# A hybrid decoder layer on one core: other PSUM pools for the projections, a rotary swap by transfers, a third plain FFN tile

## The chip, the cores and the metric

The kernel runs on one core of a Trainium2 chip. The metric is the device time of one execution in microseconds (us). Times of before are the median of three runs; the profile is of one further execution. Engines: PE (TensorE, matmuls), DVE (VectorE), ACT (ScalarE), POOL (GpSimd), SP (SyncE, whose queue issues the DMAs).

## The reference

One decode step plus a prompt of 1024 positions through one layer (all in float32). The prompt and the 8 decode positions are handled as one matrix of 1032 columns.

```python
def mixer_prompt(xn, w_in, w_out, ...):
    qkv, z, xbc, dt_raw = split_mix(xn @ w_in)
    for g, (window, dil) in enumerate(ATTN_PATTERNS):      # 3 patterns, dilation 1, 4, 16
        q = rope(qkv[..., g, 0, :, :], pos)
        k = rope(qkv[..., g, 1, :, :], pos)
        o, lse = dilated_window_prompt(q, k, qkv[..., g, 2, :, :], dil)
...
    attn = merge_patterns(outs, lses)                      # softmax over the three lse
    xs, Bm, Cm, dt, A = ssd_branch_inputs(causal_conv_silu(xbc_pad, ...), dt_raw, dt_bias, a_log)
    y, h_new = ssd_chunked(xs, dt, A, Bm, Cm)              # 8 chunks x 2 groups
    ssm = ssd_gate_out(y, xs, z, d_skip, ssd_norm_w)       # y * silu(z), RMSNorm
    return concatenate([attn, ssm], -1) @ w_out, ...
...
    yp = yp + rmsnorm(mix, norm_mix_post[l])
    yp = yp + rmsnorm(swiglu(rmsnorm(yp, norm_ffn_pre[l]), w_ffn_in[l], w_ffn_out[l]), norm_ffn_post[l])
```

The decode positions go the same way, with attention over the cached keys (`mixer_sample`), and the caches are copied to the outputs.

## The kernel before, in words

**Products.** Weights and activations are each split into a high and a low part; a product is three matmuls (high by high, low by high, high by low) for each of 8 slices of the inner dimension. One *unit* (`unit`, line 168, matmul on line 175) is these 24 matmuls into one accumulator of 344 columns; a weight tile has three units, for the column ranges c = 0, 1, 2. `gps` (line 182) gives the accumulators, going in turn through the list `gpools` of PSUM pools. In the three attention patterns and in z that list is `[psg]`, two buffers. `gemm` (line 189) loads a weight tile and runs its units; an ACT copy takes each accumulator out (line 586 in the patterns, into the tile `rw`).

**Stages, in order of units.** The conv projections XBC (units 0 to 36), attention patterns 0, 1, 2 (36 to 72, 72 to 108, 108 to 144), z (144 to 168), the output projection and its norms (168 to 204), the plain tiles of the FFN (from 204), its Strassen-like tiles (`blocks`, matmuls on line 1206: a tile of 1032 columns by 7 products of 12 matmuls of 258 columns, for each of two halves), the second FFN product and the tail.

**A pattern** is 12 weight tiles: for each of four pairs of heads (hp) v, q and k (`do_v`, `do_qk`), then `attend`, 8 steps j. `do_qk` swaps the rotary halves: four ACT copies of 32 x 1032 (line 615) make `sw` from `rw`, POOL multiplies it with the sines (line 616), DVE multiplies `rw` with the cosines (617) and adds both (620, 621). In `attend` the transposed probabilities go from PSUM to `pt` by ACT in 24 of the steps (line 671), else by DVE (673).

**Beside the patterns** run the SSD (`ssd`, from line 475; 16 groups: 8 chunks by 2) and the decode scores (`dec_scores(g)`, lines 731 to 757, after pattern g in the code). An SSD group loads `xg`, `bg` and the broadcast sums `e` (1 x 512 KB), and on DVE makes `xdt` (500), `xdd` (501), `gm` (507), 8 subtractions on `e` (516), `e*gm` (519), `eb*yo` (534), `xg+yp` (536) and `hst+stp` (542). All its PSUM tiles (`xt`, `gb`, `yp`, `yo`, `stp`), those of `dec_scores` (`rtp`, `stp`), and `pnp` and `wtp` (line 842) come from `side_ps`, the pool pss of two buffers. The *merge* of the patterns (lines 842 to 860) weights the three outputs and gives the attention part of the output projection its input.

**The norm stage.** `att_part(c)` adds the attention part to the output projection and lays two steps in the list `ahead`: `Norms.first` (statistics, first RMSNorm, residual) and `Norms.second` (second RMSNorm, the FFN's input `fh`, `fl`). They are carried out a number of units later, which the table `GAP` sets (line 27); so plain FFN tiles on c = 0, 1 run while the norm of c = 2 is worked out. `x_sums` and `w_blocks` (lines 1131 to 1190) make the sums and weight combinations that the Strassen-like tiles need.

**Order.** A scheduler sets each engine's program order when the kernel is built, from dependencies and priorities (`prio`: evac, w, side, late, main). The pools, though, hand out buffers in code order: a tile gets the buffer of the tile that was taken from its pool two before it in the code (with two buffers), and may be written only when that one's last reader is done.

Of the kernel before, what the change touches and what calls it, by code (L numbers as in the profile page):

```python
# [26 lines left out]
GAP = ((1, 3), (1, 4), (2, 6))  # L27
# [22 lines left out]
def trunk(tc, a, o):  # L50
# [558 lines left out]
    def do_qk(g, hp, which):  # L609
        rw = proj_raw(g * 12 + 4 * which + hp)  # L610
        with prio("side"):
            sw = swpp.tile([P, 3 + T], F32, tag="swp", name="sw")
            for q in range(4):
                s = q ^ 1
                nc.scalar.copy(sw[q * 32:(q + 1) * 32, 0:T], rw[s * 32:(s + 1) * 32, :])  # L615
            nc.gpsimd.tensor_tensor(out=sw[:, 0:T], in0=sw[:, 0:T], in1=sin, op=ALU.mult)  # L616
            nc.vector.tensor_tensor(out=rw, in0=rw, in1=cos, op=ALU.mult)
            qp = krp if which else qrp
            qr = qp.tile([P, S], F32, tag="qr", name="qr")
            nc.vector.tensor_tensor(out=pview(qr, g), in0=porder(rw, g), in1=porder(sw, g), op=ALU.add)  # L620
# [314 lines left out]
    gpools.append(psa)  # L935
# [54 lines left out]
    def stat(x, first, acc):  # L990
        if first:
            nc.scalar.activation(out=acc, in_=x, func=AF.Square)
# [12 lines left out]
    class Norms:  # L1005
# [12 lines left out]
        def first(self, prev):  # L1018
            c0, c1 = self.c0, self.c1
            with prio("evac"):  # L1020
                r = np_.tile([P, CW], F32, tag="nr", name="nr", bufs=1)
                finish(self.acc, r, prev=prev)
                self.acc = np_.tile([P, CW], F32, tag="nacc", name="nacc2")
                self.h = []
                for i in range(3):
# [4 lines left out]
                    for m in range(3 * i, 3 * i + n):  # L1030
                        mv, h = mix[m][:, c0:c1], self.h[m]
                        nc.vector.tensor_tensor(out=mv, in0=mv, in1=r, op=ALU.mult)
                        nc.vector.scalar_tensor_tensor(out=h, in0=mv, scalar=nw(MIX_POST, m), in1=h, op0=ALU.mult,  # L1033
                                                       op1=ALU.add)
                        stat(h, m == 0, self.acc)
                    nc.sync.dma_start(out=h_d[3 * i:3 * i + n, :, c0:c1].rearrange("k p t -> p k t"), in_=x[:, :n])

        def second(self, prev):
            c0, c1 = self.c0, self.c1
            with prio("evac"):  # L1040
                r = np_.tile([P, CW], F32, tag="nr", name="nr2", bufs=1)
                finish(self.acc, r, prev=prev)
                for m in range(KT):
# [4 lines left out]
                    nc.vector.tensor_tensor(out=fl[m][:, c0:c1], in0=mv, in1=fh[m][:, c0:c1], op=ALU.subtract)  # L1048
# [9 lines left out]
    def att_part(c):  # L1058
# [9 lines left out]
        ahead.extend([(GAP[c][0], nm.first), (GAP[c][1], nm.second)])  # L1068
# [5 lines left out]
    att_part(2)  # L1074
# [18 lines left out]
    def plain(t, c, w):  # L1093
# [5 lines left out]
        with prio("evac"):  # L1099
            s = np_.tile([P, T], F32, tag="fs", name="fs", bufs=2)[:, :CW]  # L1100
            nc.scalar.activation(out=s, in_=pg, func=AF.Silu)
# [48 lines left out]
    wslots = [(mixp, "mix")] * 8 + [(whp, "wh"), (wlp, "wl"), (whp, "wh"), (wlp, "wl")]  # L1150
# [45 lines left out]
    def blocks(t, s, w):  # L1196
# [26 lines left out]
        with prio("evac"):  # L1223
            add(u2, p1, b)
        b = prod("b22")
        with prio("evac"):
            add(v, u2, b)
        b = prod("t3")
        with prio("evac"):
            add(u3, u2, b)  # L1230
        b = prod("t4")
        with prio("evac"):
            next_copy(add(up[:, 0], u3, b))
        b = prod("t1")
        with prio("evac"):
            add(gate[:, 1], v, b)
            add(up[:, 1], u3, b)
# [10 lines left out]
    def hid_load(t):  # L1248
        with prio("w"):
            hr = np_.tile([P, T], F32, tag="xr", name="hr", bufs=3)  # L1250
# [10 lines left out]
    def ffn_out(gi):  # L1261
# [36 lines left out]

        def ev(m, c, ps):
# [20 lines left out]
        def put(c, m, r):  # L1320
# [3 lines left out]
            nc.vector.tensor_tensor(out=fv, in0=fv, in1=r, op=ALU.mult)  # L1324
# [12 lines left out]
        for c, (c0, c1) in enumerate(CL):  # L1337
            for m in range(KT):
# [30 lines left out]
    for t in range(2, HT):  # L1369
        w = w_blocks(t)  # L1370
# [101 lines left out]
```

## Time and profile before

| what | value |
|---|---|
| runs, us | 1889.53, 1892.22, 1893.98; median 1892.22 |
| profiled execution, us | 1887.21; its span on the core 1885.4 |
| granted TensorE clock, mean | 0.975 |
| PE, DVE, ACT, POOL busy, us | 1776.3, 1151.1, 781.9, 323.0 |
| last eight SSD groups, start of their xdt, us from start | 433.8 to 555.9 |
| dec_scores(0), first copy of its rows to its stp, us from start | 573.66 to 603.84 |
| last projection of z | 967.7 |
| norm stage (first att_part to first Strassen-like product) | 1037 to 1209 |

The page of the profile gives busy time by engine, the span in 40 slices, the DMA queues, the chain that ended last, the costliest groups of instructions and the DMA issues. A row of a group reads: line, engine, operation, output and inputs by tile name, shape, count, busy time, mean duration in ns, the idle time just before and who ended it. The views of windows give busy time by engine (with the number of instructions), the granted clock and the DMA share for a stretch.

### The profile page before, as it was taken

What the parts mean: (1) busy time and instruction counts of PE and PEld (TensorE: products, weight loads), DVE (VectorE), ACT (ScalarE), POOL (GpSimd) and SP (SyncE); (2) the same over time, 40 slices, a digit from 0 to 9 for tenths busy, and PEclk for the clock granted to TensorE, in tenths of its full rate; (3) what the DMA queues carried; (4) which work ended last, traced back from release to release, by engine and by line L of the source; (5) the groups of instructions that cost most, each with busy time, mean ns of one, the idle gap of its engine ahead of it and who ended that gap; (6) DMA issues with size and microseconds to landing.
All of it is one profiled execution on the core that took longest, in us unless ns stands there. A gap on an engine that the chain in (4) does not pass through costs nothing.

```text
span 1885.4 us, 30770 instructions
## 1 busy us (share of the span) xinstructions
PE 1776.3 (94%) x12207; PEld 1658.5 (88%) x12207; DVE 1151.1 (61%) x2247; ACT 781.9 (41%) x1436; POOL 323.0 (17%) x218
## 2 busy tenths in 40 slices
PE   8999989999998899999789995999999999999995
PEld 6999877888887788988678995899999999999995
DVE  6545667677765544456676699766666665532338
ACT  5533454555554555565242345432232232531133
POOL 0000244544224311133542210000000000000020
PEclk9999999999999999999979998999999999999998
DMA  4322333443325333445755443354544445886686
GB/s 158 133 95 83 104 118 117 139 135 114 99 88 180 114 118 108 148 160 192 190 148 163 128 160 124 118 174 170 171 165 170 172 162 184 314 295 205 214 305 202
DMA packets 135056, 298.61 MB, mean 158 GB/s; under 512 B 18416, under 2 KB 85200, under 8 KB 133504
## 3 DMA queue, kind: packets, MB, share of 16 engines
q1 hardware_dynamic: 134912, 296.64, 47.6%
q8 instruction: 96, 1.57, 0.3%
q14 instruction: 48, 0.39, 0.1%
HBM read 247.49 MB, written 137.10 MB: 204 GB/s over the span
## 4 chain that ended last, share of the span: by engine, by line
PE 38%; DVE 7%; DMA 3%; issue 1%; ACT 1%; POOL 1%; SPq 0%; DVEq 0%; POOLq 0%; ACTq 0%
PE fb L1206 21%; PE g L175 15%; DMA nt<-n_d 2%; PE pg L175 1%; POOL nt L855 1%; DMA hr<-hid_d 1%; DVE xr L1033 1%; PE pu L175 1%; DVE nt L856 1%; DVE nacc L996 1%; DVE sl L925 0%; DVE wl L164 0%; DVE mix L1045 0%; DVE nt L857 0%; DVE fl L1048 0%
## 5 line engine op out<-in xcount | busy, mean ns | idle before, releaser
L175 PE MATMUL g<-xh,wh 128*128 128x344 f32 x1344 | 442.9, 330 | 9.2 <-ACT rw L586 4.9
L175 PE MATMUL g<-xl,wh 128*128 128x344 f32 x1344 | 439.8, 327 | 1.5 <-DVE xl L231 1.5
L175 PE MATMUL g<-xh,wl 128*128 128x344 f32 x1344 | 438.4, 326 | 0.5 <-DVE wl L164 0.5
L175 PEld LDWEIGHTS g<-xh,wh 128*128 128x128 f32 x1344 | 255.3, 190 | 18.9 <-ACT rw L586 7.3
L175 PEld LDWEIGHTS g<-xh,wl 128*128 128x128 f32 x1344 | 255.6, 190 | 12.3 <-issue 11.0
L175 PEld LDWEIGHTS g<-xl,wh 128*128 128x128 f32 x1344 | 255.6, 190 | 10.6 <-issue 7.7
L1206 PE MATMUL fb<-fh,wsl 128*128 128x258 f32 x1280 | 234.6, 283 | 0.9 <-DVE wsl L1176 0.8
L1206 PEld LDWEIGHTS fb<-fh,wsl 128*128 128x128 f32 x1280 | 198.0, 189 | 1.5 <-DVE wsl L1176 0.9
L1206 PE MATMUL fb<-fl,wsl 128*128 128x258 f32 x640 | 180.8, 283 | 0.0
L164 DVE TENSOR_TENSOR wl<-wr,wh 128x1024 fp32r<-128x1024 f32 (+1 forms) x93 | 114.1, 1227 | 82.6 <-ACT wh L163 82.4
L175 PE MATMUL g<-hh,wh 128*128 128x344 f32 x432 | 137.4, 320 | 0.7 <-ACT wh L163 0.7
L175 PE MATMUL g<-hh,wl 128*128 128x344 f32 x432 | 137.7, 319 | 0.2 <-DVE wl L164 0.2
L175 PE MATMUL g<-hl,wh 128*128 128x344 f32 x432 | 137.3, 320 | 0.0
L163 ACT CAST wh<-wr 128x1024 fp32r<-128x1024 f32 (+1 forms) x93 | 92.5, 995 | 106.6 <-PE g L175 97.3
L660 ACT ACTIVATE sm<-sm,ngm 128x128 f32<-128x128 f32 (+1 forms) x192 | 84.9, 443 | 107.5 <-DVE ngm L656 99.5
L1288 POOL TENSOR_TENSOR ow<-wr,ow 128x512 fp32r<-128x512 f32 x8 | 10.2, 1299 | 686.3 <-ACT ow L1287 686.3
L1206 PEld LDWEIGHTS fb<-fl,wsl 128*128 128x128 f32 x640 | 120.9, 189 | 0.0
L616 POOL TENSOR_TENSOR sw<-sw,sin 128x1032 f32<-128x1032 f32 x24 | 75.8, 3157 | 250.8 <-ACT sw L615 187.3
L615 ACT COPY sw<-rw 32x1032 f32<-32x1032 f32 x96 | 101.0, 1052 | 1.4
L1210 DVE TENSOR_TENSOR fo<-fp,fb 128x258 f32<-128x258 f32 x160 | 63.7, 419 | 57.4 <-PE fb L1206 57.2
L586 ACT COPY rw<-g 128x344 f32<-128x344 f32 x108 | 47.2, 443 | 113.2 <-PE g L175 70.6
L175 PEld LDWEIGHTS g<-hh,wh 128*128 128x128 f32 x432 | 80.9, 188 | 1.1 <-ACT wh L163 1.0
(362 smaller groups left out, 3759.7 us busy)
## 6 DMA issues: line engine op xcount, KB each, us to landing
out_skv<-in_cache SPq DMA_DIRECT2D x64, 1023.5 KB, 5.5
wr<-in_w_in SPq DMA_DIRECT2D x56, 512.0 KB, 3.7
out_skv<-in_cache SPq DMA_DIRECT2D x16, 1022.0 KB, 5.5
wr<-in_w_out SPq DMA_DIRECT2D x24, 512.0 KB, 3.6
hr<-hid_d SPq DMA_DIRECT2D x22, 516.0 KB, 5.0
hid_d<-fo SPq DMA_DIRECT2D x40, 258.0 KB, 3.1
wg<-in_w_fin SPq DMA_DIRECT2D x20, 512.0 KB, 5.5
wu<-in_w_fin SPq DMA_DIRECT2D x20, 512.0 KB, 3.6
```

The lines of the kernel that those rows point to most:

```text
L163: nc.scalar.copy(wh[:, :cols], wr[:, :cols])
L164: nc.vector.tensor_tensor(out=wl[:, :cols], in0=wr[:, :cols], in1=wh[:, :cols], op=ALU.subtract)
L175: last = nc.tensor.matmul(ps, x[:, ws], y[:, c0:c1], start=(k == 0 and j == 0), stop=(k == n - 1 and j == 2))
L586: return nc.scalar.copy(rw[:, c0:c1], ps)
L615: nc.scalar.copy(sw[q * 32:(q + 1) * 32, 0:T], rw[s * 32:(s + 1) * 32, :])
L616: nc.gpsimd.tensor_tensor(out=sw[:, 0:T], in0=sw[:, 0:T], in1=sin, op=ALU.mult)
L660: nc.scalar.activation(out=sm[:, h, :nk], in_=sm[:, h, :nk], func=AF.Exp, scale=SCALE, bias=ngm[:, g, j, i:i + 1], accum_out=den[:, g, j, ...
L855: nc.gpsimd.tensor_tensor(out=nt, in0=nt, in1=wt, op=ALU.mult)
L856: nc.vector.tensor_tensor(out=nt[:, 0], in0=nt[:, 0], in1=nt[:, 1], op=ALU.add)
L996: nc.vector.tensor_tensor(out=acc, in0=acc, in1=sq, op=ALU.add)
L1206: nc.tensor.matmul(ps, x[:, ks], y, start=(k == 0 and j == 0), stop=(k == 3 and j == 2))
L1210: return nc.vector.tensor_tensor(out=dst, in0=x, in1=y, op=ALU.add)
```

## The change

- In the code ahead of `dec_scores(0)` the list of accumulators is set to `[psg, psg, pss, pss]`, and after z to `[psg, psa]`. So in patterns 1 and 2 and in z two of four accumulators in a row come from pss.
- The rotary swap is by four DMAs on SP's queue in place of the four ACT copies, and the sine product moves from POOL to DVE.
- All copies to `pt` are on ACT.
- `Norms.first` is cut in two (`first`, `resid`); `GAP` has three numbers a range; the residual's first statistic stands behind the last silu; `x_sums` and the first `w_blocks` are issued after the last norm.
- Three plain tiles in place of two; the Strassen-like ones start at t = 3.
- In `blocks` the product t1 comes after t2, no longer last; the weight slots `wslots` start with the other pools; the first two `hid_load` take another pool; the last writes stand behind a sum.

```diff
-GAP = ((1, 3), (1, 4), (2, 6))
+GAP = ((1, 1, 3), (1, 1, 4), (2, 4, 8))
...
-        return q.tile([P, 512], F32, tag="ap", name=name)[:, :cw]
+        return q.tile([P, 512], F32, tag="sp" if q is pss else "ap", name=name)[:, :cw]
...
-                nc.scalar.copy(sw[q * 32:(q + 1) * 32, 0:T], rw[s * 32:(s + 1) * 32, :])
-            nc.gpsimd.tensor_tensor(out=sw[:, 0:T], in0=sw[:, 0:T], in1=sin, op=ALU.mult)
+                nc.sync.dma_start(out=sw[q * 32:(q + 1) * 32, 0:T], in_=rw[s * 32:(s + 1) * 32, :])
+            nc.vector.tensor_tensor(out=sw[:, 0:T], in0=sw[:, 0:T], in1=sin, op=ALU.mult)
...
-            if j % 2 and j % 4 < 2:
-                nc.scalar.copy(dst, tp[:, :2 * nk])
-            else:
-                nc.vector.tensor_copy(dst, tp[:, :2 * nk])
+            nc.scalar.copy(dst, tp[:, :2 * nk])
...
+    gpools[:] = [psg, psg, pss, pss]
+    ngp[0] = 0
     with prio("side"):
         dec_scores(0)
...
-    gpools.append(psa)
+    gpools[:] = [psg, psa]
...
-        ahead.extend([(GAP[c][0], nm.first), (GAP[c][1], nm.second)])
+        ahead.extend(zip(GAP[c], (nm.first, nm.resid, nm.second)))
...
-    wslots = [(mixp, "mix")] * 8 + [(whp, "wh"), (wlp, "wl"), (whp, "wh"), (wlp, "wl")]
+    wslots = [(whp, "wh"), (wlp, "wl"), (whp, "wh"), (wlp, "wl")] + [(mixp, "mix")] * 8
...
-    pw = [(load_w(a["w_fin"][0], 1024), load_w(a["w_fin"][HT], 1024)), (far_weights(1), far_weights(HT + 1))]
-    for t, c in ((0, 0), (0, 1), (1, 0), (1, 1)):
-        plain(t, c, pw[t])
+    pw = [(load_w(a["w_fin"][0], 1024), load_w(a["w_fin"][HT], 1024))]
+    pw += [(far_weights(t), far_weights(HT + t)) for t in (1, 2)]
+    for t in range(3):
+        for c in range(2):
+            plain(t, c, pw[t])
...
-        x_sums(s)
-    for t in range(2):
+        with tc.issue_after(nm.end.ins):
+            x_sums(s)
+    for t in range(3):
         plain(t, 2, pw[t])
...
-    for t in range(2, HT):
-        w = w_blocks(t)
+    for t in range(3, HT):
+        if t == 3:
+            with tc.issue_after(nm.end.ins):
+                w = w_blocks(t)
+        else:
+            w = w_blocks(t)
```

How PE's order changes at the end of the SSD and at dec_scores(0) (`stp` from line 539 is an SSD group's state, the last one here; `g` the accumulator of a projection; `rtp` and the `stp` with `scs0` are dec_scores(0)). Before, dec_scores(0) lies within the projections and the attention of pattern 1, from unit 97.6 on:

```order
L175 MATMUL g_5839<-xh4_116,wh_5808 128x344
L175 MATMUL g_5839<-xh4_116,wl_5809 128x344
L739 MATMUL rtp_4654<-ident_90,dec0_404 8x128 x4
L680 MATMUL nps_5553<-pt_5567,vt_5257 64x128 x4
L667 MATMUL ptp_5585<-ident_90,sm_5579 128x128
L739 MATMUL rtp_4660<-ident_90,dec1_405 8x128 x4
L667 MATMUL ptp_5585<-ident_90,sm_5579 128x128
L175 MATMUL g_5839<-xl4_124,wh_5808 128x344
```

With the change the last SSD group, dec_scores(0) and the first of the pss accumulators:

```order
L497 MATMUL xt_2760<-ident_90,xg_2754 128x128 x4
L503 MATMUL gb_2769<-bg_2756 128x128
L504 MATMUL gb_2769<-ident_90,bg_2756 128x128
L523 MATMUL yp_2789<-e_2758,xdt_2765 64x128 x8
L531 MATMUL yo_2799<-bg_2756,hst_1745 128x128 x4
L539 MATMUL stp_2808<-xdd_2766,bt_2773 128x512
L736 MATMUL rtp_4654<-ident_90,dec0_404 8x128 x4
L736 MATMUL rtp_4660<-ident_90,dec1_405 8x128 x4
L736 MATMUL rtp_4666<-ident_90,dec2_406 8x128 x4
L751 MATMUL stp_4723<-ident_90,scs0_4674 32x128 x2
L752 MATMUL stp_4723<-bones_4646,prod_4650 32x2
L175 MATMUL g_4788<-xh0_112,wh_4731 128x344
```

Ahead of these rows stand, since unit 76.0, the last six attention steps of pattern 0 and seven more SSD groups, and no row of line 175. Before, the stp of dec_scores(0) stands at unit 102.5.

DVE's order with the change, one SSD group in that stretch (before, rows of attention, of weight splits and of the rotary products stand between):

```order
L542 TENSOR_TENSOR hst_1745<-hst_1745,stp_2518 128x512
L516 TENSOR_SCALAR e_2584<-e_2584,cs_1655 128x128 x8
L500 TENSOR_TENSOR xdt_2533<-xt_2528,dt_1650 128x512
L501 TENSOR_TENSOR xdd_2534<-xt_2528,dtd_1656 128x512
L507 TENSOR_TENSOR gm_2540<-gb_2537,tri_426 128x128
L519 TENSOR_TENSOR e_2526<-e_2526,gm_2540 128x1024
L534 TENSOR_TENSOR eb_2544<-eb_2544,yo_2567 128x512
L536 TENSOR_TENSOR xg_2522<-xg_2522,yp_2557 128x512
L542 TENSOR_TENSOR hst_1745<-hst_1745,stp_2576 128x512
```

The subtractions on the tile `e_2584` of the group after next stand ahead of this group's `xdt`.

PE's order at the first `wtp` of the merge, before, within z's projections:

```order
L175 MATMUL g_9172<-xl6_126,wh_9115 128x344
L175 MATMUL g_9172<-xh7_119,wh_9115 128x344
L842 MATMUL wtp_8464<-ident_90,wo_8463 64x128 x3
L175 MATMUL g_9172<-xh7_119,wl_9116 128x344
L175 MATMUL g_9172<-xl7_127,wh_9115 128x344
```

With the change:

```order
L667 MATMUL ptp_8286<-ident_90,sm_8280 128x128 x2
L677 MATMUL nps_8245<-pt_8289,vt_7953 64x128 x2
L878 MATMUL nps_8637<-cvt_8638,sel_8634 8x512
L878 MATMUL nps_8637<-cvt_8650,sel_8634 8x512
L841 MATMUL wtp_8464<-ident_90,wo_8463 64x128
L175 MATMUL g_8809<-xh0_112,wh_8752 128x344
```

The first `wtp` stands at unit 148.0, right behind dec_scores(2) and the last eight attention steps, with none of z's projections among them.

## Rows read from the trace of the kernel before

**Rows 1.** Page, busy time, share and count of each engine.
```profile
PE 1776.3 (94%) x12207; PEld 1658.5 (88%) x12207; DVE 1151.1 (61%) x2247; ACT 781.9 (41%) x1436; POOL 323.0 (17%) x218
```

**Rows 2.** Windows: stretch, length, busy PE, PEld, DVE, ACT, POOL, clock, DMA, GB/s.
```profile
94.00:141.00 47.00, 47.00 (x301) 47.00 (x301) 21.13 (x26) 18.41 (x26) 0.40 (x4) 1.00 0.27 96
...
422.00:604.00 182.00, 176.80 (x1252) 151.25 (x1251) 122.52 (x287) 94.17 (x195) 66.55 (x44) 0.98 0.39 123
604.00:850.00 246.00, 240.06 (x1642) 213.46 (x1640) 113.88 (x305) 138.21 (x307) 52.26 (x25) 0.99 0.39 130
850.00:970.00 120.00, 101.21 (x565) 84.69 (x563) 75.76 (x131) 48.35 (x90) 50.94 (x32) 0.91 0.62 179
...
1037.00:1209.00 172.00, 142.77 (x830) 138.67 (x830) 142.30 (x265) 75.85 (x142) 17.73 (x7) 0.91 0.38 123
1209.00:1607.00 398.00, 397.99 (x3316) 397.99 (x3317) 259.76 (x476) 112.58 (x161) 0.00 (x0) 1.00 0.51 175
```

**Rows 3.** Waits of PE: what waited for what, total us, times, longest us.
```profile
PE pg L175 <- ACT fs L1101: 18.3, 1, 18.3
...
PE g L175 <- ACT rw L586: 4.9, 6, 1.7
```

**Rows 4.** Line 500 from 420 to 560 us: durations in ns, first and last start.
```profile
L500 DVE TENSOR_TENSOR xdt<-xt,dt x8: 678/691/692, 433.8 to 555.9; 128x512 f32<-128x512 f32 x8
```

**Rows 5.** DMA issues from 422 to 604 us: count, KB each, median us to landing.
```profile
e<-cs_d SPq DMA_DIRECT2D x6, 512.0 KB, 3.9
```

**Rows 6.** Groups by line on DVE from 422 to 560 us.
```profile
L652 DVE CUSTOM_DVE_ANT_0 sm<-sps,mask 128x256 f32<-128x256 f32 (+1 forms) x38 | 12.6, 367 | 1.6 <-PE ptp L667 1.0 <-PE sps L646 0.5
L519 DVE TENSOR_TENSOR e<-e,gm 128x1024 f32<-128x1024 f32 x8 | 11.1, 1392 | 0.1
L516 DVE TENSOR_SCALAR e<-e,cs 128x128 f32<-128x128 f32 x48 | 10.8, 295 | 1.2 <-ACT eb L513 1.2
...
L673 DVE COPY pt<-ptp 128x512 f32<-128x512 f32 (+1 forms) x15 | 8.5, 564 | 3.4 <-PE ptp L667 3.4
...
L500 DVE TENSOR_TENSOR xdt<-xt,dt 128x512 f32<-128x512 f32 x8 | 5.5, 688 | 3.1 <-PE xt L497 2.8
...
L507 DVE TENSOR_TENSOR gm<-gb,tri 128x128 f32<-128x128 f32 x8 | 2.3, 283 | 1.0 <-PE gb L504 1.0
```

**Rows 7.** Groups by line on ACT from 422 to 560 us.
```profile
L660 ACT ACTIVATE sm<-sm,ngm 128x256 f32<-128x256 f32 (+1 forms) x40 | 18.5, 463 | 21.6 <-DVE ngm L656 15.3 <-PE xt L497 6.0
...
L513 ACT ACTIVATE eb<-e 64x512 f32<-64x512 f32 x12 | 7.5, 628 | 7.3 <-POOL xg L535 4.2 <-DMA e<-cs_d 3.0
```

**Rows 8.** Timeline of PE, last SSD group: start, duration.
```profile
562.38 1.09 PE L523 MATMUL yp<-e,xdt 128*64 128x128 f32 x16
```

**Rows 9.** Timelines of ACT, POOL and PE in dec_scores(0).
```profile
573.66 1.05 ACT L740 COPY rows<-rtp 8x512 f32<-8x512 f32 x2
...
592.94 3.36 POOL L616 TENSOR_TENSOR sw<-sw,sin 128x1032 f32<-128x1032 f32 x1
...
603.84 0.59 PE L754 MATMUL stp<-ident,scs 128*32 128x128 f32 x2
```

**Rows 10.** Timeline of PE around z; in brackets idle time before, and its releaser.
```profile
855.40 0.39 PE L754 MATMUL stp<-ident,scs 128*32 128x128 f32 x2 [2.00 <-DVE scs L750]
...
906.83 0.57 PE L842 MATMUL wtp<-ident,wo 128*64 128x128 f32 x3 [0.51 <-DVE wo L841]
...
970.20 0.94 PE L955 MATMUL g<-sh,wh 128*128 128x344 f32 x2 [2.03 <-ACT sh L924]
```

**Rows 11.** Windows in the norm stage, columns as in rows 2.
```profile
1160.00:1180.00 20.00, 2.69 (x9) 2.69 (x10) 16.46 (x41) 11.12 (x24) 0.00 (x0) 0.60 0.25 88
```

**Rows 12.** Page, costliest groups, and line 617: the rotary products.
```profile
L616 POOL TENSOR_TENSOR sw<-sw,sin 128x1032 f32<-128x1032 f32 x24 | 75.8, 3157 | 250.8 <-ACT sw L615 187.3
L615 ACT COPY sw<-rw 32x1032 f32<-32x1032 f32 x96 | 101.0, 1052 | 1.4
...
L617 DVE TENSOR_TENSOR rw<-rw,cos x24: 1218/1233/3462, 207.1 to 833.8; 128x1032 f32<-128x1032 f32 x24
```

More of the change, by code (lines that the diff above doesn't have):

```diff
@@ L988, in trunk, with stat @@
     fl = [actp.tile([P, T], F32R, tag="act", name=f"fl{k}") for k in range(KT)]
-    def stat(x, first, acc):
+    silu = []
+    def stat(x, first, acc, prev=None):
         if first:
-            nc.scalar.activation(out=acc, in_=x, func=AF.Square)
+            ins = nc.scalar.activation(out=acc, in_=x, func=AF.Square)
+            if prev is not None:
+                behind(ins, prev)
         else:
@@ L1022, in first, with resid @@
                 finish(self.acc, r, prev=prev)
+                self.r = r
+        def resid(self, prev):
+            c0, c1 = self.c0, self.c1
+            with prio("evac"):
+                r = self.r
                 self.acc = np_.tile([P, CW], F32, tag="nacc", name="nacc2")
@@ L1034, in first @@
                                                        op1=ALU.add)
-                        stat(h, m == 0, self.acc)
+                        stat(h, m == 0, self.acc, silu[-1] if silu and m == 0 else None)
                     nc.sync.dma_start(out=h_d[3 * i:3 * i + n, :, c0:c1].rearrange("k p t -> p k t"), in_=x[:, :n])
@@ L1047, in second @@
                     nc.scalar.copy(fh[m][:, c0:c1], mv)
-                    nc.vector.tensor_tensor(out=fl[m][:, c0:c1], in0=mv, in1=fh[m][:, c0:c1], op=ALU.subtract)
+                    self.end = nc.vector.tensor_tensor(out=fl[m][:, c0:c1], in0=mv, in1=fh[m][:, c0:c1], op=ALU.subtract)
     ahead = []
@@ L1067, in att_part @@
             step(last, .5)
-        ahead.extend([(GAP[c][0], nm.first), (GAP[c][1], nm.second)])
+        ahead.extend(zip(GAP[c], (nm.first, nm.resid, nm.second)))
+        return nm
     att_part(0)
@@ L1073, in trunk @@
         step(gemm(a["w_out"][m][:, 512:1536], 1024, sh, sl, ssm_ev(m), cc=(2,), share=True))
-    att_part(2)
+    nm = att_part(2)
     right.close()
@@ L1100, in plain @@
             s = np_.tile([P, T], F32, tag="fs", name="fs", bufs=2)[:, :CW]
-            nc.scalar.activation(out=s, in_=pg, func=AF.Silu)
+            silu.append(nc.scalar.activation(out=s, in_=pg, func=AF.Silu))
             next_copy(nc.vector.tensor_tensor(out=s, in0=s, in1=pu, op=ALU.mult))
@@ L1224, in blocks @@
             add(u2, p1, b)
+        p5 = prod("t1")
+        with prio("evac"):
+            add(v, u2, p5)
         b = prod("b22")
         with prio("evac"):
-            add(v, u2, b)
+            add(gate[:, 1], v, b)
         b = prod("t3")
@@ L1230, in blocks @@
             add(u3, u2, b)
+            add(up[:, 1], u3, p5)
         b = prod("t4")
@@ L1233, in blocks @@
             next_copy(add(up[:, 0], u3, b))
[L1234 to L1237, printed above, removed]
             nc.scalar.activation(out=gate, in_=gate, func=AF.Silu)
@@ L1249, in hid_load @@
         with prio("w"):
-            hr = np_.tile([P, T], F32, tag="xr", name="hr", bufs=3)
+            hr = (rowp.tile([P, T], F32, tag="row", name="hr") if t < 2
+                  else np_.tile([P, T], F32, tag="xr", name="hr", bufs=3))
             nc.sync.dma_start(out=hr, in_=hid_d[t])
@@ L1297, in ffn_out @@
         accs = [acct[:, c0:c1] for c0, c1 in CL]
+        summed = [None]
         def ev(m, c, ps):
@@ L1307, in ev @@
                 nc.scalar.activation(out=sq[:, :c1 - c0], in_=fv, func=AF.Square)
-                nc.vector.tensor_tensor(out=acc, in0=acc, in1=sq[:, :c1 - c0],
-                                                                                 op=ALU.add)
+                summed[0] = nc.vector.tensor_tensor(out=acc, in0=acc, in1=sq[:, :c1 - c0], op=ALU.add)
             nc.scalar.activation(out=fv, in_=fv, func=AF.Copy, scale=nw(FFN_POST, m))
@@ L1318, in out_unit, with put @@
             return last
-        def put(c, m, r):
+        def put(c, m, r, prev=None):
             c0, c1 = CL[c]
             fv = fac[m][:, c0:c1]
-            nc.vector.tensor_tensor(out=fv, in0=fv, in1=r, op=ALU.mult)
+            ins = nc.vector.tensor_tensor(out=fv, in0=fv, in1=r, op=ALU.mult)
+            if prev is not None:
+                behind(ins, prev)
             if c < 2:
@@ L1348, in ffn_out @@
                         for i in ((m - 2,) if m < KT - 1 else (m - 2, m - 1, m)):
-                            put(c - 1, i, r)
+                            put(c - 1, i, r, summed[0])
         with prio("evac"):
```

## The prediction

> **What bounds the kernel now.** I read the engine totals first: TensorE (PE) is busy 94% of the span, VectorE (DVE) 61% [rows 1]. Then the windows by stage [rows 2]: PE has almost no idle time from 94 us to 850 us (47.00 of 47, 176.80 of 182, 240.06 of 246 us) and none in the Strassen-like tiles (397.99 of 398). What it loses it loses around z (101.21 of 120) and in the norm stage (142.77 of 172), and there the granted clock also falls, to 0.91. The waits of PE [rows 3] agree: the longest single one, 18.3 us, is at the second FFN tile, behind a ScalarE (ACT) result that is late because of the norms; the wait for a projection accumulator to be copied out, which the four accumulators aim at, is 4.9 us in all. So the kernel is bound by PE, in PE's own order, and what counts is where PE's queue will hold nothing that can run.
>
> The profiled execution took 1887.2 us; the sum below is made against that. It stands 5.0 us under the median of the runs, 1892.2, so 5 us are added at the end.
>
> **Unit prices.** A projection matmul of 344 columns costs 47.00/301 = 0.156 us [rows 2], a unit of 24 of them 3.75 us. A Strassen-like tile of 168 matmuls costs 398 x 168/3316 = 20.2 us [rows 2]; a plain tile of six units 22.5 us.
>
> **1. Accumulators on pss, pattern 1: +90 us.** The pools hand out their buffers in code order. The SSD and dec_scores take all their PSUM tiles from pss, and pss has two. An accumulator of pattern 1 on pss can be written only when the last tile of SSD and dec_scores(0) on pss has been read. The order shows it: four units of pattern 1 on psg come early, then from unit 76.0 on no L175 row stands until dec_scores(0)'s stp is past. Before, 26.1 units stand in that place, and they kept PE busy in the window 422 to 604 [rows 2]. Now there are left, with no projection beside them: six attention steps, eight SSD groups, three rtp and stp.
>
> How long is that stretch? By pieces:
> - Six attention steps. One is two masked maxima of 0.37, two exponentials of 0.46 and a copy of 0.56 [rows 6, 7], one behind the other 2.2 us; with its matmuls and small operations I take 3.3: 20 us (bounds 0, all beside the SSD, and 30).
> - Eight SSD groups. DVE's order puts the eight subtractions L516 of the group after next ahead of the next group's xdt. Their e tile is loaded into the buffer that this group's yp has just read. So one group follows the other by a ring: load of e 3.9 us [rows 5], eb 2 x 0.63 [rows 7], L516 8 x 0.30, xdt and xdd 0.69 each, gm 0.28, e*gm 1.39 [rows 6], yp 1.09 [rows 8]: together 11.7 us. Six groups at 11.7 and the last two, which load nothing more, at about 8: 86 us. Lower bound: DVE's own work, 2.4 + 1.4 + 0.3 and five operations like xdt = 7.5 a group, 60 us. Upper bound: the spacing of before, (555.9 - 433.8)/7 = 17.4 us [rows 4], 139 us; there the groups shared DVE and ACT with attention, so I take the ring.
> - dec_scores(0). Before it took 603.84 - 573.66 = 30.2 us from its first copy to stp, 3.4 of them behind a POOL sin product [rows 9] that moves away: 27 us (24 to 30).
>
> Sum 20 + 86 + 27 = 133 us (84 to 189; 60 + 24 below). Then the 26.1 units have to run. In the window 604 to 850 [rows 2], 46.2 units took 246 us with the attention of their patterns between them, 5.32 each, and that attention is still to come: 139 us (at the bare 3.75 it would be 98, but the attention doesn't vanish). Before, all of it took 182: 133 + 139 - 182 = +90 us.
>
> **2. The same at z: +10 us.** z's accumulators on pss wait for dec_scores(2), pnp and the first wtp. At unit 148 PE's order holds stp, eight attention steps, pnp, nps and wtp with no projection among them. Before, it was 51.4 us from stp (855.40, after a wait of 2.00) to wtp (906.83) with projections between [rows 10]. Alone I take 47, then 20 units x 3.75 = 75, then the 7 us it now takes to the first L955: 129. Before, the last 20 units and that step took from about 851 to 970.20: 119. So +10; a chain of 30 us would make it -7, one of 51 with some of the units behind it at half clock +23.
>
> **3. dec_scores(1), in pattern 2: +4 us** (0 to 12). Its stp stands at unit 112.0, before 112.3; it is only the projections that lay ahead of it which are now behind. DVE and POOL are no longer late there, so a small stall.
>
> **4. Shorter waits for an accumulator: -3 us** (0 to -5): rw 4.9 us is all there is to win [rows 3].
>
> **5. Third plain tile, three-part norms: -29 us.** From the first att_part to the first Strassen-like product before: 172 us [rows 2] for 32 units = 120 us of PE at full speed. The difference is DVE: busy 142.30 of 172 [rows 2], and PE did 2.69 of 20 us of work in 1160 to 1180, at a clock of 0.60 [rows 11]. The 18.3 us wait [rows 3] lies there. Now six plain units (c = 0, 1) cover the last norm instead of four, x_sums and w_blocks come behind it, and one Strassen-like tile of 20.2 becomes a plain one. PE's work is 38 units = 142.5; I leave it 10 us behind DVE, 8 for x_sums and w_blocks and 2.5 of half clock: 163, against 172 + 20.2: -29. If only 7.5 us of idle time stay, -42; if DVE keeps all its lead, 183 and -9.
>
> **6. The rest: 0.** The 96 ACT copies (1.05 us each) and the POOL sin products [rows 12] go; 96 DMAs of 132 KB on SP and 24 DVE products, each like L617's 1.23 us [rows 12], come: 30 us of DVE over 650 us in which it is busy 60% or less and PE is the bound. The copies to pt moving from DVE to ACT give 0.56 us a step back to DVE; ACT, 41% busy [rows 1], loses the 101 us of swap copies. PE's lead covers all that; without it, see rival three. The order of wslots, of the product t1, the buffer of hid_load and the order of the last writes lie in stretches in which PE doesn't wait [rows 2] or in the tail, and I give them nothing (-3 to +3).
>
> Sum: +90 + 10 + 4 - 3 - 29 = +72: 1959 profiled, **1964 us** as a median.
>
> **A rule weighed.** The windows show six accumulator banks used in turn at a clock of 1.00, the level of 2.4 GHz, with no idle time (94 to 141) and eight in the Strassen-like tiles, also 1.00 [rows 2]. The Trainium skill, "TensorE: Matmul & The Clock Gate", section "A second HAM failure mode: psum-queue depth-cycling", says that a kernel which cycled through PSUM banks in each iteration idled briefly between its groups of matmuls so often that the clock swung between its levels. By the rows four banks cost nothing; by that rule the sum would be that of rival four. This case's trace speaks against it.
>
> **Rivals.**
> - *One, faster or the same (0.08).* The pieces of the stretch overlap: attention goes beside the SSD, e is loaded early enough and the groups run at DVE's 7.5 us. Place: from unit 76 to dec_scores(0)'s stp. The stretch is 84 us and costs 84 + 139 - 182 = +41; with terms 2 to 5 at their best (-7, 0, -5, -42) that is -13: 1879 us. It decides below 93 us of stretch, and only with all of these. For it: 7.5 us of DVE [rows 6]; against it: DVE's order, which holds the ring.
> - *Two, slower still (0.15).* The groups keep 17.4 us [rows 4], because SP's queue delays e and y: 139 + 20 + 27 = 186, +143 in place of +90: 2017 us.
> - *Three (0.10).* SP is in order: each swap DMA waits there until rw is copied out, and the weight loads stand behind it. Before, ACT did that without holding a load. If each of 24 swaps holds the next load by 2 us and PE runs dry, +48: 2012 us. For it: no weight load is in SP's order between that of unit 76 and the end of the stretch.
> - *Four (0.05).* The brief pauses between accumulators make the clock swing. If a tenth of the 72 x 24 = 1728 projection matmuls of patterns 1 and 2 runs at the lower level of the clock, 1.2 GHz, 0.156 us more each would be 27 us: 1991 us.
> - That the change doesn't do what it says: two pools in place of one give no lead if the next accumulator always waits for pss; then term 4 is 0, which the range holds.
>
> **How the numbers follow.** My forecast has 0.62. Its own range is 1964 with the stretch at 105 to 160 us and terms 2 and 5 at their bounds, not all at once: about 1920 to 2000. Rival two lies above, rival one below. The range **1912 to 2012** leaves out rival one, rival two and some of the tails: about 0.2. 0.2% (4 us) is about what a measurement of this kernel can tell from no change. Faster by more: 0.05 (most of rival one); within: 0.03; slower: 0.92.
>
> **What would show it.** Right: after about 425 us a stretch of some 130 us with hardly an L175 matmul, PE's granted clock low in it, xdt (L500) every 11 to 12 us, and the first pss accumulator right behind stp; a second, shorter one before wtp; 5.3 us a unit after it; no 18 us wait at the second FFN tile. Wrong: if projections run between the SSD groups, if the stretch is under 95 us, or if PE is idle before weight casts (rival three).

## The result: slower, and the profile after

The changed kernel takes 1982.0 us (median of 4 runs, 1981.2 to 1985.9), before 1893.1 on the same chip: ratio 1.0467, 95% interval 1.0431 to 1.0504. The forecast was 1964 with a range of 1912 to 2012. The profiled execution took 1981.3 us, 94.1 more than that of before.

Page of the changed kernel, busy time by engine, and the granted clock in 40 slices:

```profile
PE 1812.5 (92%) x12183; PEld 1683.8 (85%) x12183; DVE 1117.3 (56%) x2180; ACT 702.5 (35%) x1403; POOL 245.2 (12%) x194
...
PEclk9999999996679999999698999999999999999998
```

Against [rows 1] DVE, ACT and POOL all have less to do; the clock has two dips, one at slices 10 to 12 and one at slice 20. The windows of the changed kernel, columns as in [rows 2], cut at the marks of the table below:

```profile
422.00:564.50 142.50, 72.28 (x380) 48.55 (x379) 67.79 (x151) 28.14 (x59) 45.40 (x40) 0.65 0.35 108
564.50:757.50 193.00, 187.75 (x1258) 168.26 (x1257) 77.34 (x195) 75.17 (x199) 11.04 (x8) 0.98 0.33 99
757.50:949.80 192.30, 184.08 (x1244) 164.72 (x1244) 82.51 (x227) 79.39 (x227) 12.25 (x8) 0.98 0.50 157
949.80:1097.00 147.20, 111.59 (x576) 93.52 (x577) 88.26 (x144) 48.69 (x97) 64.32 (x38) 0.82 0.63 179
1097.00:1164.00 67.00, 66.33 (x394) 64.36 (x393) 35.62 (x37) 21.62 (x24) 9.41 (x4) 0.96 0.29 99
1164.00:1326.00 162.00, 154.11 (x929) 150.24 (x928) 143.39 (x264) 76.18 (x142) 12.74 (x5) 0.97 0.44 142
1326.00:1705.00 379.00, 379.00 (x3162) 379.00 (x3161) 252.40 (x457) 109.91 (x157) 0.00 (x0) 1.00 0.51 172
```

In the first window PE is busy half the time at a clock of 0.65; before it had 176.80 of 182 there [rows 2]. The same work can be followed by marks, the start of one PE instruction each (us from the span's start):

| mark | before | changed | lost so far |
|---|---|---|---|
| stp of dec_scores(1), unit 112 | 665.1 | 757.6 | +92.5 |
| stp of dec_scores(2) | 855.4 | 949.8 | +94.4 |
| output projection, first (L955, now L954) | 970.2 | 1097.3 | +127.1 |
| first att_part matmul (`ah`, `wah`) | 1044.6 | 1164.3 | +119.7 |
| first Strassen-like product (`fb`) | 1207.4 | 1325.9 | +118.5 |
| end of the span | 1885.4 | 1979.5 | +94.1 |

So 94 us are lost up to dec_scores(2), 33 more up to the output projection, and 33 come back behind it, 24 of them after the first `fb`, where one Strassen-like tile is missing.

Timeline of PE in the changed kernel, in the first stretch (in brackets idle time before and its releaser):

```profile
436.81 1.10 PE L497 MATMUL xt<-ident,xg 128*128 128x128 f32 x4 [1.45 <-DMA xg<-xs_d]
...
453.70 1.98 PE L523 MATMUL yp<-e,xdt 128*64 128x128 f32 x16 [4.79 <-issue]
455.61 1.97 PE L531 MATMUL yo<-bg,hst 128*128 128x128 f32 x8
...
535.47 2.49 PE L736 MATMUL rtp<-ident,dec 128*8 128x128 f32 x12 [1.22 <-DVE xg L536]
564.10 0.59 PE L751 MATMUL stp<-ident,scs 128*32 128x128 f32 x2 [26.13 <-issue]
564.61 0.27 PE L752 MATMUL stp<-bones,prod 128*32 128x2 f32 x2
564.81 0.65 PE L175 MATMUL g<-xh,wh 128*128 128x344 f32 x1
```

The last projection before it starts at 422.5; the last attention steps and eight SSD groups go by without a projection, the steps ending beside the first group, dec_scores(0) waits 26 us for its chain of DMAs and products, and the next projection, on pss, stands right behind stp. From 422.5 to 564.8 are 142 us.

The second one, PE's waits from 940 to 1100 us (total us, times, longest):

```profile
PE g L175 <- DVE wl L164: 8.5, 2, 4.2
PE nps L878 <- DVE cvt L877: 8.4, 5, 3.8
PE stp L751 <- DVE scs L747: 6.1, 1, 6.1
PE nps L878 <- DVE sel L864: 5.0, 1, 5.0
PE ptp L930 <- POOL acc L917: 4.9, 1, 4.9
PE wtp L841 <- DVE wo L840: 3.1, 1, 3.1
```

The projections start again at 979.07, right behind wtp, but then don't run through: they wait for weights (wl) and, in PE's order, behind the merge's matmuls (nps from cvt).

### The profile page after: what moved, and what is told of

It reads as the page before. It is cut to its first block, busy times and chain, and to the rows that moved or that the text cites. A ratio compares the mean times of both kernels' runs of the same rounds, so it can differ in the third digit from the quotient of the medians.

```text
span 1979.5 us, 30821 instructions
## 1 busy us (share of the span) xinstructions
PE 1812.5 (92%) x12183; PEld 1683.8 (85%) x12183; DVE 1117.3 (56%) x2180; ACT 702.5 (35%) x1403; POOL 245.2 (12%) x194
## 4 chain that ended last, share of the span: by engine, by line
PE 39%; DVE 6%; DMA 3%; issue 1%; POOL 1%; ACT 1%; SPq 0%; DVEq 0%; POOLq 0%; ACTq 0%
PE fb L1216 19%; PE g L175 15%; PE pu L175 2%; DMA nt<-n_d 2%; PE pg L175 2%; DMA cvt<-in_cache 1%; PE g L954 1%; DVE nacc L999 1%; POOL nt L854 1%; DVE nt L855 0%; DVE mix L1054 0%; DVE wl L164 0%; DVE xr L1042 0%; DVE fac L1340 0%; DVE al L858 0%
## 5 line engine op out<-in xcount | busy, mean ns | idle before, releaser
L1216 PE MATMUL fb<-fh,wsl 128*128 128x258 f32 x1216 | 222.2, 283 | 0.0
L1216 PEld LDWEIGHTS fb<-fh,wsl 128*128 128x128 f32 x1216 | 188.1, 189 | 0.0
L1216 PE MATMUL fb<-fl,wsl 128*128 128x258 f32 x608 | 172.1, 283 | 0.0
L164 DVE TENSOR_TENSOR wl<-wr,wh 128x1024 fp32r<-128x1024 f32 (+1 forms) x93 | 109.1, 1174 | 94.2 <-ACT wh L163 93.9
L163 ACT CAST wh<-wr 128x1024 fp32r<-128x1024 f32 (+1 forms) x93 | 92.5, 996 | 115.7 <-PE g L175 111.2
L652 DVE CUSTOM_DVE_ANT_0 sm<-sps,mask 128x128 f32<-128x128 f32 (+1 forms) x192 | 59.1, 348 | 109.9 <-PE ptp L667 71.1
L1216 PEld LDWEIGHTS fb<-fl,wsl 128*128 128x128 f32 x608 | 115.0, 189 | 0.0
L670 ACT COPY pt<-ptp 128x256 f32<-128x256 f32 (+1 forms) x96 | 45.3, 472 | 103.6 <-PE ptp L667 103.2
```

What stands on the lines that cost most here:

```text
L163: nc.scalar.copy(wh[:, :cols], wr[:, :cols])
L164: nc.vector.tensor_tensor(out=wl[:, :cols], in0=wr[:, :cols], in1=wh[:, :cols], op=ALU.subtract)
L652: nc.vector.tensor_tensor_reduce(out=sm[:, h, :nk], in0=sps[h][:, c0:c0 + nk], in1=msk, scale=1.0, scalar=0.0, op0=ALU.add, op1=ALU.max, a ...
L1216: nc.tensor.matmul(ps, x[:, ks], y, start=(k == 0 and j == 0), stop=(k == 3 and j == 2))
```

## The experiments

All are against the kernel before on the same chip; its median was 1889.6 to 1892.6 us on the chips used here and 1893.1 on that of the result above, so a difference between runs of two chips carries up to some 3 us. Where the reason of a time is read from marks, these are the marks of the table above.

**x1_no_pss**: the pools undone, the rest kept.

```diff
-    gpools[:] = [psg, psg, pss, pss]
-    ngp[0] = 0
```

> The changed kernel, but the accumulators of patterns 1, 2 and z on psg alone as before; everything else of the change stays. Theory (pool order): the two stretches without projections, at unit 76 and at unit 148, go, and with them the +94 us up to dec_scores(2) and the +25 us around z; what stays is the gain of the norm stage and the third plain tile: 1981 - 119 = 1862 us (1850 to 1872). Rival (SP queue: swap DMAs hold weight loads): a good part of the loss stays, over 1890 us.

1871.4 us (ratio 0.9893, 0.9866 to 0.9921). This is at the upper end of what was expected. The pools cost 1982.0 - 1871.4 = 110.6 us of the changed kernel (107 when each is taken against before on its own chip). dec_scores(2)'s stp stands at 867.1, still 11.7 behind before, so the swap or the copies to pt cost something too.

**x2_only_pss**: the kernel before with the pools alone (the lines above added, the name of the tile's tag, and the list set to `[psg, psa]` behind z).

> The kernel before with the list of accumulators alone changed as in the change; swap by ACT copies, norms and tiles as before. Theory (pool order): the same two stretches in PE's order, so before + 94 + 25 = 2006 us (1990 to 2020), slower than the changed kernel. Rival (the loss needs the swap DMAs): 1950 us or less.

2003.1 us (1.0587, 1.0567 to 1.0607): +113, and nothing else of the change is in it. The pool order is shown from both sides. Its stp of dec_scores(1) stands at 745.3, +80 against before; in the changed kernel the other 12 come from the other parts. Window of x2 over the stretch:

```profile
422.00:557.00 135.00, 69.46 (x377) 46.43 (x376) 64.99 (x154) 25.27 (x56) 42.60 (x38) 0.64 0.35 110
```

**x4_pss_z**: x1 with the pools set ahead of z alone.

```diff
+    gpools[:] = [psg, psg, pss, pss]
+    ngp[0] = 0
     yg = []
     for k in range(KT):
```

> As x1_no_pss, but z's accumulators are psg, psg, pss, pss. Theory: only the second stretch (wtp at unit 148.0) comes back: x1_no_pss + 25 us = about 1887 (1875 to 1897), and z's weight loads come late behind the merge's loads on SP. Rival (z's part was a consequence of the first stretch, work pushed together): within 8 us of x1_no_pss.

1903.9 us (1.0067, 1.0047 to 1.0086), 32.5 over x1, above what was expected. z's loss needs no first stretch.

**x5_pss_from_hp3**: x1 with the pools set late, and back to psg for z.

```diff
         for hp in range(HP):
+            if g == 1 and hp == 3:
+                gpools[:] = [psg, psg, pss, pss]
+                ngp[0] = 0
...
+    gpools[:] = [psg]
+    ngp[0] = 0
     yg = []
```

> As x1_no_pss, but accumulators psg, psg, pss, pss from the last head pair of pattern 1 (unit 99) through pattern 2; z on psg. Theory (pool order): four accumulators cost nothing by themselves; the first one on pss comes only shortly ahead of dec_scores(0)'s stp at unit 103, so the stall is small: x1_no_pss + 0 to 18 us. Rival (cycling through four banks lets the clock swing or slows PE): pattern 2 runs at over 5.6 us a unit and the sum is over x1_no_pss + 20 us.

1885.1 us (0.9967, 0.9946 to 0.9988), 13.7 over x1. z is on psg here, so the loss to compare with is 110.6 - 32.5 = 78 us: moving where in the code the pools are set by 27 units takes most of it away. Four accumulators don't slow PE: window of pattern 2, from dec_scores(1)'s stp to dec_scores(2)'s, of x5 and, with two accumulators, of x1:

```profile
682.00:879.00 197.00, 194.81 (x1315) 174.94 (x1315) 84.32 (x228) 85.28 (x234) 11.55 (x8) 0.99 0.52 166
```

```profile
671.00:867.00 196.00, 192.00 (x1301) 171.84 (x1299) 83.78 (x235) 86.31 (x238) 11.85 (x8) 0.99 0.51 163
```

The clock is 0.99 in both.

**x8_pool_order**: what spaces the SSD groups in the stretch; the changed kernel with POOL's two operations in the other order.

```diff
-            nc.gpsimd.tensor_tensor(out=xf, in0=xf, in1=ef, op=ALU.add)
+            added = nc.gpsimd.tensor_tensor(out=xf, in0=xf, in1=ef, op=ALU.add)
...
-            nc.gpsimd.tensor_tensor(out=v64(hst[:, g]), in0=v64(hst[:, g]), in1=b64(cdk), op=ALU.mult)
+            behind(nc.gpsimd.tensor_tensor(out=v64(hst[:, g]), in0=v64(hst[:, g]), in1=b64(cdk), op=ALU.mult), added)
```

> The changed kernel with one order changed: in an SSD group POOL adds eb to xg (line 535) before it scales the state (line 541), so eb's buffer is free 1.04 us sooner. If the ring that spaces the groups in the stretch goes through eb and POOL (spacing of xdt 12.5 us in the changed kernel), the spacing falls to about 12.0 us and the stretch by 4 us. If it goes through the load of e, as the prediction had it, it stays at 12.5 us.

1990.3 us, one run; its stretch starts 11 us later than in the changed kernel, and the spacing is what counts here. The mean spacing of xdt is (533.0 - 449.1)/7 = 12.0 us, which is what the way through eb and POOL would give, but the number misleads: the first and the last gap, 10.6 each, make it. The five between are 12.3 to 12.8, mean 12.56; the same five of the changed kernel have a mean of 12.74 (all seven 12.5). So the groups came 0.2 us closer, not 0.5. The rows tell why. One group in the changed kernel, timeline of all engines:

```profile
468.40 0.33 SPq L492 DMA_DIRECT2D e<-cs_d  x1
...
470.37 0.69 DVE L534 TENSOR_TENSOR eb<-eb,yo 128x512 f32<-128x512 f32 x1 [4.12 <-PE yo L531]
470.41 1.04 POOL L541 TENSOR_TENSOR hst<-hst,cdk 128x512 f32<-128x512 f32 x1 [7.49 <-PE yo L531]
...
471.41 1.26 POOL L535 TENSOR_TENSOR xg<-xg,eb 128x512 f32<-128x512 f32 x1
472.71 0.63 ACT L513 ACTIVATE eb<-e 64x512 f32<-64x512 f32 x1 [7.42 <-POOL xg L535]
```

and in x8:

```profile
464.68 0.33 SPq L492 DMA_DIRECT2D e<-cs_d  x1
467.55 1.26 POOL L535 TENSOR_TENSOR xg<-xg,eb 128x512 f32<-128x512 f32 x1 [8.30 <-DVE eb L534]
468.85 0.63 ACT L513 ACTIVATE eb<-e 64x512 f32<-64x512 f32 x1 [6.40 <-POOL xg L535]
```

Line 541 ran beside DVE's L534 anyway and stood only 0.3 us in the way of L535, not 1.04; the expectation was worked out too large. But the two ways can be told apart. In both kernels eb starts 0.04 us behind the end of L535, which the profile names as its releaser. The load of e, issued 4.2 to 4.3 us before, is done by then: the last of its 128 packets of 4 KB in the trace's DMA records ends at 471.50 in the changed kernel and at 467.91 in x8, 1.2 and 0.9 us before eb. Where the profile does name the load as releaser, as in x8's first group at 456.76, eb starts 0.4 us behind the last packet. In the five groups of the changed kernel where the profile names L535 the packets end 0.6 to 1.3 us before eb, so the way from yo over L534 and L535 to eb's buffer sets the spacing there, and the load would let the groups come some 0.2 to 0.9 us closer.

**x10_both_back, x6_swap_copies, x9_pt_back**: the swap and the copies to pt, each with x1's pools. x6 takes back the swap, x9 the sharing of pt, x10 both:

```diff
-                nc.sync.dma_start(out=sw[q * 32:(q + 1) * 32, 0:T], in_=rw[s * 32:(s + 1) * 32, :])
-            nc.vector.tensor_tensor(out=sw[:, 0:T], in0=sw[:, 0:T], in1=sin, op=ALU.mult)
+                nc.scalar.copy(sw[q * 32:(q + 1) * 32, 0:T], rw[s * 32:(s + 1) * 32, :])
+            nc.gpsimd.tensor_tensor(out=sw[:, 0:T], in0=sw[:, 0:T], in1=sin, op=ALU.mult)
...
-            nc.scalar.copy(dst, tp[:, :2 * nk])
+            if j % 2 and j % 4 < 2:
+                nc.scalar.copy(dst, tp[:, :2 * nk])
+            else:
+                nc.vector.tensor_copy(dst, tp[:, :2 * nk])
```

> As x1_no_pss, but the rotary swap is by ACT copies with the sine product on POOL and the copies to pt are shared out as before: what stays of the change is the norm stage, the third plain tile, the product order, the buffers and the last writes. PE's order up to the norm stage is that of before again (dec_scores at units 102.5, 112.3, 149.7). Theory (x1's markers: +11 us up to dec_scores(2) from swap or pt, -26 from the norms on): before - 26 = about 1864 us (1857 to 1868), 8 to 11 us under x1_no_pss. Rival (the 11 us are the other order of work, not those two): within 3 us of x1_no_pss.

> As x1_no_pss, but only the swap is back on ACT copies with the sine product on POOL; the copies to pt all on ACT. If the swap DMAs on SP cost the 11 us (weight loads behind them): as x10_both_back, about 1864 us. If the copies to pt on ACT cost it (PE's attention waits for ACT): it stays at 1871 or is worse, since ACT then carries both, 1871 to 1885 us.

> As x1_no_pss, but only the copies to pt are shared out between DVE and ACT as before; the swap by DMAs. If the pt copies cost the 11 us: about 1862 us; if the swap DMAs cost it: about 1871 us.

| | pt shared out | pt all on ACT |
|---|---|---|
| swap by ACT copies | x10: 1859.7 (0.9844, 0.9829 to 0.9859) | x6: 1884.6 (0.9974, 0.9962 to 0.9987) |
| swap by DMAs | x9: 1868.2 (0.9886, 0.9871 to 0.9901) | x1: 1871.4 |

x10 is the best of all, 30 us under before, as expected. x6 falls into the case against the copies to pt, x9 nearer the case against the swap, so neither edit alone is the cost. The two are not additive: with the copies to pt on ACT the swap by DMAs gains 13 us, with them shared out it costs 8.5. Nor does the cost fall where the edits are: in x6, which loses 25 us against x10, stp of dec_scores(2) is 10.7 us later (865.8 against 855.1), the output projection's first matmul 4.6 (976.0 against 971.4), but the first att_part matmul 24.9 (1070.6 against 1045.7), where no attention is left. What moved is the merge: each edit gives the scheduler another order, and in x6's the merge's first wtp stands at unit 161.8 and starts at 930.2, in x10's at 158.9 and 907.0. Behind it the output projection waits for weights, 10.9 us in place of 3.4. Why the other orders cost what they do before that point is not shown. It is not that PE waited for weight loads behind the swap DMAs: PE's waits from 188 us to dec_scores(2) hold no wait for a weight in x1 or x9.

**x11_two_plain**: x10 with two plain tiles and the old distances of the norms.

```diff
-GAP = ((1, 1, 3), (1, 1, 4), (2, 4, 8))
+GAP = ((1, 1, 3), (1, 1, 4), (2, 2, 6))
...
-    for t in range(3):
-        for c in range(2):
+    for t in range(2):
+        for c in range(2):
...
-    for t in range(3, HT):
-        if t == 3:
+    for t in range(2, HT):
+        if t == 2:
```

> As x10_both_back, but with two plain tiles and the norms at the distances of before (residual right behind the first norm, second norm of the last range after six plain units); x_sums and w_blocks still behind the last norm, product order and buffers as changed. If the third plain tile is what covers the last norm: the wait at a plain tile behind the norms comes back (18 us before), one Strassen-like tile (20.2) takes the place of a plain one (22.5): x10_both_back + 16 to 22 us, 1876 to 1882. If the order of the sums and the norms made the gain: within 6 us of x10_both_back.

1883.3 us (0.9957, 0.9941 to 0.9973). Each against before on its own chip, x10 gains 30 us and x11 9, so 21 lie between them, within what was expected. The tile and the distances were taken back together, so the run doesn't tell them apart. PE's waits in the norm stage of x11:

```profile
PE pg L175 <- ACT fs L1112: 10.8, 1, 10.8
PE fb L1217 <- ACT wsl L1186: 6.5, 1, 6.5
```

The wait at a plain tile [rows 3] is back, shorter, and one at the first Strassen-like product is new. In x10 neither is there. Windows of x10 over the same stretches as [rows 2] and [rows 11]:

```profile
1037.00:1209.00 172.00, 165.82 (x1031) 163.19 (x1030) 146.05 (x267) 80.73 (x149) 17.78 (x8) 0.98 0.42 141
1160.00:1180.00 20.00, 18.96 (x119) 18.42 (x118) 15.42 (x29) 11.70 (x23) 0.00 (x0) 1.00 0.47 159
```

DVE does 146 us there in place of 142, but PE 166 in place of 143, at a clock of 0.98 in place of 0.91.

**x12_merge_pool_queue, x12_merge_act_queue**: x4 with the merge's loads on another queue; the edit is that of POOL's, the other has `nc.scalar`.

```diff
-                nc.sync.dma_start(out=nt, in_=n_d[:, hp, :, qs]...
+                nc.gpsimd.dma_start(out=nt, in_=n_d[:, hp, :, qs]...
...
-                    nc.sync.dma_start(out=wt[h * 64:(h + 1) * 64],
+                    nc.gpsimd.dma_start(out=wt[h * 64:(h + 1) * 64],
```

> As x4_pss_z, but the merge's loads of nt and wt are issued by POOL's queue in place of SP's. If z is held because SP's queue has the merge's loads (which wait for POOL) ahead of the loads of cvt and of z's weights: from dec_scores(2)'s stp to the first attention part of the output projection, 219 us in x4_pss_z, falls to 205 or less. If it is the merge's own work on POOL and DVE beside z: it stays at 214 or more.

> The same with the merge's loads issued by ACT's queue. The same two cases: 205 us or less if SP's order holds z, 214 or more if the merge's work does (or if ACT, waiting for the merge's buffers, now holds z's own copies zt).

From stp to the first att_part matmul: 219.3 us in x4, 200.2 on POOL's queue (1881.9 us, one run), 214.7 on ACT's (1897.2, one run). By the expectation SP's order holds z in the first and not in the second. But the totals hide two moves. Windows from the first wtp to the output projection, in x4, on POOL's queue and on ACT's:

```profile
891.90:1018.40 126.50, 95.34 (x501) 85.25 (x502) 78.29 (x86) 39.51 (x63) 60.30 (x34) 0.85 0.56 159
897.60:993.80 96.20, 88.50 (x499) 80.51 (x499) 68.17 (x65) 35.66 (x56) 68.09 (x59) 0.94 0.60 155
902.40:1010.90 108.50, 91.16 (x500) 83.14 (x500) 61.81 (x72) 38.75 (x60) 50.08 (x28) 0.89 0.58 164
```

So z's 20 units ran 30 and 18 us shorter without the merge's loads in SP's queue, and PE's waits for zt are gone in both. Ahead of wtp 8 and 10 us were given back: from stp to wtp it is 25.5 us in x4, 33.4 and 35.9 here. On ACT's queue one more pair of the merge's products (nps) stands ahead of wtp and waits 6.7 us for cvt there, so some 8 of the 18 us have only changed sides. SP's order holds z in both runs, by 30 and some 10 us; left of that in the stage are 19 and 5 of the 32 us. Why ACT's queue frees less is not shown. Timeline of SP in the changed kernel:

```profile
1006.19 0.55 SPq L148 DMA_DIRECT2D wr<-in_w_in  x1
...
1020.88 0.38 SPq L849 DMA_DIRECT2D nt<-n_d  x1
1021.35 1.23 SPq L852 DMA_DIRECT2D wt<-w_d  x2
1023.22 0.33 SPq L148 DMA_DIRECT2D wr<-in_w_in  x1
...
1038.36 0.37 SPq L849 DMA_DIRECT2D nt<-n_d  x1
1038.78 0.58 SPq L852 DMA_DIRECT2D wt<-w_d  x1
1040.46 0.35 SPq L148 DMA_DIRECT2D wr<-in_w_in  x1
```

and SP's waits from 949 to 1100 us:

```profile
SPq L852 <- POOL nt L854: 33.4, 11, 5.7
```

A weight tile of z comes every 17 us, behind loads of the merge that wait for POOL; three units need 11.25.

**x13_best_pool_queue**: x10 with that queue.

> x10_both_back with the merge's loads of nt and wt on POOL's queue. Here z's projections are spread before the merge, and PE waits for the merge's work only 6 to 10 us between dec_scores(2) and the output projection. If SP's order with the merge's loads ahead costs also here: 1848 to 1855 us. If it only costs where z comes after the merge's start: within 4 us of x10_both_back, 1856 to 1864.

1873.6 us (0.9903, 0.9880 to 0.9925), some 13 us slower than x10. z ends sooner (output projection at 965.4, x10 971.4), but a new wait of 14.9 us stands before att_part, for the weights `wah`. Neither case of the expectation holds: in this kernel, where most of z comes ahead of the merge, the other queue costs.

## Why the prediction was right, and where its terms were off

The sign, the mechanism and the range held: the order of the pools puts a stretch of 142 us without projections into PE's queue, x1 and x2 show it from both sides (+111 and +113), and x5 that the place in the code decides. The sum of +72 fell 22 short of the +94 profiled: terms 1, 2 and 6 were too small, term 3 had the wrong sign, and the errors in part cancel.

- **Term 1, +90, and term 3, +4.** To dec_scores(1)'s stp the changed kernel lost 92.5 us, 94 with the third of a unit it lies behind. The pieces of the stretch: attention 14 us (422.5 to 436.8, forecast 20), SSD 99 (436.8 to 535.5, forecast 86), dec_scores(0) 29 (forecast 27), 142 together in place of 133. The 36 units behind took 193 us, 5.36 each (5.32 forecast). Split at unit 102.5, term 1 was 142 + 26.5 x 5.36 - 181 = +103. Term 3 was -10: the units from 102.5 to 112.3 took 61 us before and run at 5.36 each now, like the others. That 94 came out for the sum of both, forecast and measured, is luck: two errors of some 13 us cancel. The pools alone (x2) lost 80; the other 12 belong to term 6.
- **The ring of the SSD groups.** They were 12.5 us apart, where the ring gave 11.7. `yp` took 1.98 us in place of 1.09 [rows 8], because PE, idle half the time there, ran mostly at the lower clock level (1.2 GHz); those 0.9 us alone would bring the ring to 12.6. But the ring's wait was the wrong one: from yp to eb the later way was not e's load but yo, L534 and POOL's L535 (x8), which the prediction didn't have. `yo` runs at the lower clock there too (1.97 us). [rows 7] could have told: before, 4.2 of the 7.3 us that ACT idled ahead of eb ended with L535, 3.0 with the load.
- **Term 2, +10.** It was +25 (127.1 - 94.4 = 33, less 7.4 by which the stage up to att_part is shorter). The pools alone gave more: +34 between the same marks in x2, 32.5 in all in x4. Part of the 33 is where the mark lies: stp stands at unit 148.0 now and stood at 149.7. Counted from unit 148, which began at 846.7 before (the prediction took 851), to the output projection it is 147.5 us against 123.5: +24, and +17 with the 7.4 taken off. The stall itself was shorter than taken: 979.1 - 949.8 = 29 us from stp to the first projection, not 47. The step that failed is the next: "then 20 units x 3.75 = 75, then the 7 us it now takes". They took 1097.3 - 979.1 = 118. Before, 15 of z's 24 units were done when the merge's wtp was reached; now four are, and the other 20 run beside the merge. z shares SP's queue with the merge's loads, and the merge's matmuls stand between z's on PE. x12 shows SP's part: 30 us behind wtp on POOL's queue, 19 of them left in the stage.
- **Term 4, -3.** The waits on rw fell from 4.9 [rows 3] to 2.2 us: right, and as small.
- **Term 5, -29.** From the first att_part matmul to the end the changed kernel gained 25.6 us, x10 29.2, and the 18.3 us wait is gone. The third plain tile, with its longer distances, carries most of it: x11, without them, gains 9.4 there. The stage took 161.6 us (forecast 163), but the 172 of before were read too wide: the first att_part matmul stands at 1044.6, not 1037, and the stage was 162.8 long. By that the forecast would have been -20; of the 5 us more, 4 came behind the first `fb`.
- **Term 6, 0.** 10.8 us in the changed kernel to dec_scores(2) (949.8 against x2's 939.0), about 12 us in the medians between x1 and x10. The step that failed is "PE's lead covers all that". It covers the busy time, which fell on ACT and POOL; that the other order is what costs is argued from x6, x9 and x10, not shown for these 12 us.

Of the rivals, one and two are out: the groups kept 12.5 us, neither 7.5 nor 17.4. Rival three's 48 us are out: the swap and the copies to pt together cost a quarter of that, and PE waits for no weight before dec_scores(2) (x1, x9). Its sign, PE idle before weight casts, did show at z (wl, 8.5 us), but there the loads stand behind the merge's, not behind swaps. Rival four is out by x5's window, clock 0.99 with four accumulators in turn. With it the rule of the Trainium skill that was weighed there ("TensorE: Matmul & The Clock Gate", "A second HAM failure mode: psum-queue depth-cycling") found nothing in this case to act on. The clock did fall, to 0.65 and 0.82, but in the stretches where PE was busy for half and three quarters of the time, waiting for other work; z's 20 units with the same four accumulators ran at 0.85 in x4 and at 0.94 in x12 on POOL's queue, where PE waits less.

## What to carry to other kernels

Buffers that a pool hands out in code order tie the work of two streams together: before a busy stream is given buffers of a pool that a slow one uses, look in the order for the first of its tiles that would have to wait for the slow one's last. Where the order moves a whole stage beside another, price that stage with the other's queues and engines in it, not at its bare rate. And an edit that only takes load off an engine that is not the bound can still cost, and the scheduler's order changes with it: x10, which leaves the pools, the swap and the copies as they were, is the version to keep.

## What had not been expected of the hardware

The prediction had the clock low in the stretch; what it left out is that the clock stayed down for the first projections behind. They ran at 0.50 (1.2 GHz) up to 570 us, and then at 1.00. Windows of the changed kernel:

```profile
564.80:570.00 5.20, 5.20 (x20) 5.19 (x19) 0.48 (x2) 0.00 (x0) 0.00 (x0) 0.50 0.17 54
570.00:575.00 5.00, 5.00 (x35) 5.00 (x34) 1.40 (x2) 1.39 (x2) 0.00 (x0) 1.00 0.20 61
```

Half of 5.2 us, 2.6, is what that costs behind the stretch; within it, the small matmuls of the SSD, priced in the ring at full clock, ran at 1.2 GHz for the most part, and `yp` alone takes 0.9 us a group more.
